# Attention values as unrounded matmuls in two column halves, one group for every four query blocks

## The chip, the cores and the metric

The kernel runs on one core of one Trainium2 chip. The metric is the device time of one execution in microseconds, the median of the runs of a kernel. Before the change that is 1438.92 us over 3 runs (1438.23 to 1439.44). Trace and page come from one further execution of the same kernel.

## The reference

One residual block on 1024 tokens of width 1024, in float32. Two branches share a normalised input; the change touches only the first of them, the stick-breaking attention with 8 heads of 64 columns:

```python
xn = rmsnorm(x, norm1_g)
q_sb, k_sb, v_sb, f_raw, i_hg, q_hg, g_hg, gate_sb, gate_hg = split(xn @ w_in)
# per head, per block of 128 queries
z = einsum('qd,kd->qk', q, k) * 64 ** -0.5
mask = kpos[None, :] < qpos[:, None]                     # strictly causal
log_beta = log_sigmoid(z)
log_rem = where(mask, log_beta - z, 0.0)
between = cumsum(log_rem, reverse=True) - log_rem
w = where(mask, exp(log_beta + between), 0.0)
o_sb = einsum('qk,kd->qd', w, v)                         # the part that changes
# the second branch: a gated linear recurrence over 4 heads of 128 (HGRN2), o_hg
merged = sigmoid(gate_sb) * (o_sb @ w_o_sb) + sigmoid(gate_hg) * (o_hg @ w_o_hg)
h = x + merged @ w_out
h = h + square(relu(rmsnorm(h, norm2_g) @ w_ff1)) @ w_ff2
out = rmsnorm(h, final_g)
```

## The kernel before

**Precision.** TensorE takes two kinds of operands here. Rounded ones (type fp32r) go through quickly but lose low bits, so a matrix is kept as a rounded part (suffix `h` or `H`, "hi") and a remainder (suffix `l` or `L`, "lo"). `hi_copy` makes the hi part with a copy on ScalarE (L144), `lo_sub` subtracts it from the source on VectorE (L149), and `hi_lo` does both. A product of two split matrices is three matmuls (hi·hi, hi·lo, lo·hi). Plain f32 operands are also taken, unrounded; the second branch uses them (tiles `sl`, `pkv`, `pho`).

**Stages.** First 58 us: the norm, the turned input `xn`, and the first projections. From 58 to 315 us: attention, 64 items (8 heads, query blocks in the order 7, 0, 6, 1, 5, 2, 4, 3), with the projections of the later heads and of the second branch filled in between ("fill"). Then the second branch, the merge, the output projection, and the two MLP products.

**One item** (head `h`, query block `qb` of 128 queries) goes through four functions. `scores` multiplies queries and keys into PSUM banks `z` and takes two sigmoids into `bt` and `rm` (ScalarE). `weights` forms the running product along the keys by a scan and multiplies it into `bt` (VectorE, L777 and L157). `turn` transposes `bt` in pieces of 128x128 on TensorE (bank `pw`, L124) and splits what comes out into `wTh` (ScalarE) and `wTl` (VectorE). `values` multiplies the turned weights with the head's values into bank `po`. The loop over items calls `weights` for the next item, `scores` for the one after it, some fill, and then `turn` of this item; `values` of a group that became complete runs in the item after that.

**Values before.** A group is a pair of query blocks, `qc` from 0 to 3, with `2*qc+2` key blocks. `v_epilogue` stores the values of a head as 64 hi columns beside 64 lo columns, so that a stationary operand of 128 columns holds both. For each key block there are two matmuls of 256 query columns, one against `wTh` and one against `wTl`: 320 matmuls in all (2+4+6+8 key blocks, times 2, times 8 heads). The upper and lower 64 rows of `po` are then added: ScalarE copies one half to `ot` (L850), VectorE adds the other (L851) into `osb`. Where the second block of a pair has one key block more than the first, `turn` has GpSimd clear the missing piece of `wTh` and `wTl` (L811).

**Order.** Each engine takes its instructions in program order. TensorE has two lanes, "main" (attention) and "fill"; a gate holds fill back until the main block two before it. `after(a, b)` only fixes an order on one engine: `turn_lo` holds the last remainder subtraction of a turn, and some scans and multiplies of `weights` are placed behind it. DMA loads are issued by SP in the order of the program; GpSimd issues the DMAs that copy QH and QL to the upper rows (L663) between its memsets.

**Memory.** Tiles of 128x1024 come from a pool of 40 slots, tiles up to 512 columns from 10 half slots; PSUM has 8 banks.

Of the kernel before, what the change touches and what calls it, by code (L numbers as in the profile page):

```python
# [9 lines left out]
F32 = mybir.dt.float32  # L10
# [9 lines left out]
P = 128  # L20
# [19 lines left out]
def kernel(  # L40
# [34 lines left out]
    def slot(name, dt=F32):  # L75
        return spool.tile([P, 1024], dt, tag="s", name=name)
# [75 lines left out]
    def hi_lo(h, l, src):  # L152
        hi_copy(h, src)
        return lo_sub(l, src, h)
# [493 lines left out]
    def v_stat(h, tb):  # L648
        c = ((tb % 2) * 4 + h % 4) * P
        return vt[h // 4, tb // 2][:, c : c + P]  # L650

    def qk_epilogue(h):
        def ep(ps, half):
# [80 lines left out]
    lastsel, turn_lo = [None], [None]  # L734

    def scores(h, qb):
        open_block("main")
# [29 lines left out]
    def weights(h, qb):  # L767

        nk = (qb + 1) * P
        bt, rm = zs[h, qb]
        cut = qb == NT - 1
        parts = ((512, nk - 1), (0, 512)) if cut else ((0, nk - 1),)
        for i, (a, b) in enumerate(parts):
            rr = rm[:, a:b][:, ::-1]
            sc = nc.vector.tensor_tensor_scan(  # L777
                out=rr,
                data0=rr,
                data1=bits[:, 1024 - nk + a : 1024 - nk + b][:, ::-1],  # L780
                initial=rm[:, b : b + 1] if i else 0.0,
                op0=ALU.mult,
                op1=ALU.max,
            )
            if i == 1 or (qb == 5 and h in (2,)):
                after(sc, turn_lo[0])
            m = mul(bt[:, a:b], bt[:, a:b], rm[:, a:b])
            if qb == 5:
                after(m, turn_lo[0])

    def turn(h, qb, between):

        open_block("main")
        bt, rm = zs.pop((h, qb))
        qc, par = qb // 2, qb % 2
        nkb = 2 * qc + 2
        if (h, qc) not in wTt:
            wTt[h, qc] = [
                tuple(
                    slot_n(f"wT{n}{h}_{qc}_{k0}", 256 * min(nkb - k0, 4), F32R).rearrange(  # L800
                        "p (k q) -> p k q", q=256
                    )
                    for n in "hl"
                )
                for k0 in range(0, nkb, 4)
            ]
        tiles = wTt[h, qc]
        qs = slice(par * P, (par + 1) * P)
        if par == 0:
            for t in tiles[-1]:  # L810
                after(nc.gpsimd.memset(t[:, (nkb - 1) % 4, qs].bitcast(F32), 0.0), lastsel[0])  # L811
        order = list(enumerate(tiles))
        for i, (th, tl) in order[::-1] if qb == NT - 1 else order:
# [13 lines left out]
            turn_hi[0] = hi_last[0]  # L827
        seen[h, qc] = seen.get((h, qc), 0) + 1
        return (h, qc) if seen[h, qc] == 2 else None

    def values(h, qc):
        open_block("main")
        tiles = wTt.pop((h, qc))
        nkb = 2 * qc + 2
        po = bank(f"po{h}_{qc}")[:, 0:256]
# [12 lines left out]
        other = DHS - r  # L848
        tmp = slot_n(f"ot{h}_{qc}", 256)[:, 0:256]
        nc.scalar.copy(tmp[r : r + DHS, :], po[other : other + DHS, :])  # L850
        nc.vector.tensor_tensor(  # L851
            out=osb[pair][r : r + DHS, qc * 256 : (qc + 1) * 256],
            in0=po[r : r + DHS, :],
            in1=tmp[r : r + DHS, :],
            op=ALU.add,
        )


    hg, ohg = {}, {}
# [101 lines left out]
    def hg_levels(h):  # L961

        dec, k, q = (hg[h, n] for n in ("pp", "k", "q"))
        sc = hg[h, "sc"] = slot(f"sc{h}")
        near = slot_n(f"near{h}", NT * Q)[:, 0 : NT * Q]
        nc.gpsimd.memset(near, 0.0)
        nc.gpsimd.memset(sc, 0.0)

        def scores_of(l, size, firsts, where):

            open_block("main")
            S = bank(f"sl{h}_{l}")
            for i, (s0, t0) in enumerate(firsts):
                r0, c0 = where(i, s0)
                matmul(
                    S[r0 : r0 + size, c0 : c0 + size],
                    k[:, s0 : s0 + size],
                    q[:, t0 : t0 + size],  # L980
                    start=True,
                    stop=True,
                )
            return S

        def near_scores(l):
# [12 lines left out]
        after(keep(5, S), turn_lo[0])  # L999
        yield  # L1000
        for l in range(7):
            H = 1 << l
            n = 512 // H
            if l < 5:
                S = near_scores(l)
            elif l == 5:
                S = scores_of(
                    l,
                    H,
                    [(s0, s0 + H) for s0 in range(0, T, 2 * H)],  # L1010
                    lambda i, s0: (s0 % P, s0 // P * H),
                )
# [12 lines left out]
            if l < 5:  # L1025
                keep(l, S)
            elif l == 5:
                for b in range(0, P, Q):
                    nc.scalar.copy(chunks(sc)[b : b + Q, :, b : b + Q], chunks(near, Q)[b : b + Q])
                for b in range(0, P, 2 * H):  # L1030
                    nc.scalar.copy(
                        chunks(sc)[b : b + H, :, b + H : b + 2 * H],
                        chunks(S[b : b + H, 0 : NT * H], H),
                    )
            else:
                for i in range(2):
# [1063 lines left out]
    for i, it in enumerate(items):  # L2100
# [150 lines left out]
```

## Time and profile before

| What | Value |
|---|---|
| median of 3 runs | 1438.92 us (1438.23 to 1439.44) |
| profiled execution | 1437.51 us, of which the span of instructions is 1435.7 us |
| granted TensorE clock | 0.998 |
| TensorE (PE) busy | 1421.1 us, 99% of the span |
| weight loads (PEld) | 1202.9 us, 84% |
| VectorE (DVE) | 1048.5 us, 73% |
| ScalarE (ACT) | 666.7 us, 46% |
| GpSimd (POOL) | 148.4 us, 10% |
| HBM | 162.55 MB read, 61.87 MB written |

Matmuls are pipelined: the time of one row runs from its start to the end of its last result, and the next one starts before that. What a matmul costs TensorE is therefore read from start to start of neighbouring rows, not from the duration of one. A plain f32 matmul stands in the trace as two records (two weight loads, two matmuls), a rounded one as one.

### The profile page before, as it was taken

Reading aid. Unit: us, or ns where it says so; the run is one execution under the profiler, and the core shown is the slowest. Engines: PE = TensorE matmul, PEld = TensorE weight load, DVE = VectorE, ACT = ScalarE, POOL = GpSimd, SP = SyncE. Lnnn points to the kernel's source line nnn. Section 1 sums busy time; section 2 is a strip of 40 time slices with the busy share of each in tenths; the row PEclk is TensorE's granted clock in tenths of the full one; section 3 lists DMA queues with packets and bytes.
Section 4 is the critical chain, followed back from the end, with each engine's and each line's share of the span. In section 5 each row is a group of like instructions: output and inputs, shape, how many; then the busy total and the mean of one; then the engine's idle time right before and its main releaser. Section 6 shows DMA issues by size and latency. Waiting matters only on the chain.

```text
span 1435.7 us, 22472 instructions
## 1 busy us (share of the span) xinstructions
PE 1421.1 (99%) x8774; PEld 1202.9 (84%) x8774; DVE 1048.5 (73%) x1432; ACT 666.7 (46%) x1164; POOL 148.4 (10%) x347
## 2 busy tenths in 40 slices
PE   9999999999999999999989999999999999999998
PEld 8989988987898888888878888888888888888886
DVE  6699899785635677877749897666666758668765
ACT  7566666542322344433335674544444433524343
POOL 3121121120001013000010300000000000000042
PEclk9999999999999999999999999999999999999999
DMA  7234154321303359754487405444446974776724
GB/s 213 49 93 110 37 95 83 60 45 53 104 16 104 91 173 259 233 170 154 154 246 275 176 30 198 140 140 142 159 154 223 344 261 161 271 274 248 271 103 180
DMA packets 157922, 225.89 MB, mean 157 GB/s; under 512 B 25676, under 2 KB 93816, under 8 KB 157816
## 3 DMA queue, kind: packets, MB, share of 16 engines
q1 hardware_dynamic: 142552, 183.29, 38.0%
q0 software_dynamic: 11520, 34.61, 9.7%
q10 hardware_dynamic: 3744, 6.56, 1.2%
q8 instruction: 69, 1.13, 0.3%
q14 instruction: 37, 0.30, 0.1%
HBM read 162.55 MB, written 61.87 MB: 156 GB/s over the span
## 4 chain that ended last, share of the span: by engine, by line
PE 95%; DMA 1%; issue 1%; POOL 1%; DVE 1%; ACT 1%; SPq 0%; POOLq 0%; DVEq 0%
PE pm L121 21%; PE pX L121 9%; PE pW L121 6%; PE pY L121 6%; PE pjqk L121 6%; PE pji L121 3%; PE pga L121 3%; PE pjq L121 3%; PE pjf L121 3%; PE pys L121 3%; PE gX L121 3%; PE pyh L121 3%; PE gY L121 3%; PE pjg L121 3%; PE po L121 3%; PE z L121 2%
## 5 line engine op out<-in xcount | busy, mean ns | idle before, releaser
L144 ACT CAST whid<-w 128x1024 fp32r<-128x1024 f32 x30 | 31.6, 1053 | 155.2 <-PE pm L121 91.0
L777 DVE TENSOR_TENSOR_SCAN rm<-rm,bits 128x511 f32<-128x511 f32 (+7 forms) x72 | 87.3, 1219 | 14.2 <-ACT rm L755 12.7
L121 PE MATMUL pm<-wlod,sh 128*128 128x512 f32 x240 | 93.5, 390 | 0.0
L121 PE MATMUL pm<-whid,sh 128*128 128x512 f32 x240 | 93.4, 389 | 0.0
L121 PE MATMUL pm<-whid,sl 128*128 128x512 f32 x240 | 93.4, 389 | 0.0
L121 PE MATMUL pm<-tl,sh 128*128 128x512 f32 (+1 forms) x210 | 81.3, 387 | 0.0
L121 PE MATMUL pm<-th,sl 128*128 128x512 f32 (+1 forms) x210 | 81.3, 387 | 0.0
L121 PE MATMUL pm<-th,sh 128*128 128x512 f32 (+1 forms) x210 | 81.3, 387 | 0.0
L149 DVE TENSOR_TENSOR wlod<-w,whid 128x1024 fp32r<-128x1024 f32 x30 | 36.7, 1223 | 57.6 <-ACT whid L144 57.3
L149 DVE TENSOR_TENSOR sl<-sa,sh 128x1024 fp32r<-128x1024 f32 x56 | 68.2, 1218 | 1.0 <-ACT sh L144 1.0
L144 ACT CAST wTh<-pw 128x128 fp32r<-128x128 f32 (+3 forms) x96 | 44.4, 487 | 52.7 <-PE pw L124 45.2
L1900 POOL TENSOR_SCALAR fss<-fss 128x1 f32<-128x1 f32 x8 | 4.5, 561 | 562.1 <-ACT fsc L1895 561.6
L144 ACT CAST sh<-sa 128x1024 fp32r<-128x1024 f32 x56 | 57.2, 1045 | 4.7 <-DMA sa<-ad 3.4
L149 DVE TENSOR_TENSOR wTl<-pw,wTh 128x512 fp32r<-128x512 f32 (+3 forms) x96 | 50.6, 547 | 9.7 <-ACT wTh L144 7.2
L121 PEld LDWEIGHTS pm<-wlod,sh 128*128 128x128 f32 x240 | 45.1, 188 | 10.0 <-DVE wlod L149 0.4
L121 PEld LDWEIGHTS pm<-whid,sl 128*128 128x128 f32 x240 | 45.1, 188 | 9.2
L121 PEld LDWEIGHTS pm<-whid,sh 128*128 128x128 f32 x240 | 45.0, 187 | 9.3
L157 DVE TENSOR_TENSOR bt<-bt,rm 128x511 f32<-128x511 f32 (+7 forms) x72 | 48.9, 685 | 5.1 <-ACT bt L758 1.0
L121 PE MATMUL pX<-sql,t1h 128*128 128x512 f32 x128 | 50.0, 391 | 0.1
L121 PE MATMUL pX<-sqh,t1h 128*128 128x512 f32 x128 | 49.8, 389 | 0.0
L121 PE MATMUL pX<-sqh,t1l 128*128 128x512 f32 x128 | 49.8, 389 | 0.0
L755 ACT ACTIVATE rm<-z 128x511 f32<-128x511 f32 (+6 forms) x96 | 47.5, 501 | 4.5 <-DVE bt L157 1.9
(912 smaller groups left out, 4486.9 us busy)
## 6 DMA issues: line engine op xcount, KB each, us to landing
w<-in_w_ff_dram SPq DMA_DIRECT2D x72, 512.0 KB, 4.9
sa<-ad SPq DMA_DIRECT2D x56, 512.0 KB, 6.6
ad<-a SPq DMA_DIRECT2D x32, 256.0 KB, 4.4
ad<-s SPq DMA_DIRECT2D x16, 512.0 KB, 5.7
tw<-in_w_out_dram POOLq DMA_DIRECT2D x24, 256.0 KB, 4.1
x<-in_x_dram SPq DMA_DIRECT2D x8, 512.0 KB, 8.5
xnl<-xnh POOLq DMA_DIRECT2D x8, 512.0 KB, 9.9
pr<-pd SPq DMA_DIRECT2D x8, 512.0 KB, 6.0
```

The costliest lines, as they stand in the source:

```text
L121: return pe(nc.tensor.matmul(*a, **k))
L144: hi_last[0] = after(in_turn("act", nc.scalar.copy(dst, src)), hi_behind[0])
L149: nc.vector.tensor_tensor(out=dst, in0=src, in1=hi.bitcast(F32), op=ALU.subtract),
L157: return nc.vector.tensor_tensor(out=out, in0=a, in1=b, op=ALU.mult)
L755: nc.scalar.activation(rm[:, s0 + c0 - 1 : s0 + m - 1], z[:, c0:m], AF.Sigmoid, scale=-0.125)
L777: sc = nc.vector.tensor_tensor_scan(out=rr, data0=rr, data1=bits[:, 1024 - nk + a : 1024 - nk + b][:, ::-1], initial=rm[:, b : b + 1] if i ...
L1900: nc.gpsimd.tensor_scalar(out=ssq, in0=ssq, scalar1=1.0 / D, scalar2=EPS, op0=ALU.mult, op1=ALU.add)
```

## The change

Values and turned weights are no longer split. `v_epilogue` copies the values as f32 (64 columns a head), `turn` copies the transposed weights as f32 into a single tile `wT`; the subtractions on VectorE and the GpSimd memsets are gone. `values` works on four query blocks at once: a big pair (`qc` 3 or 2) and the small one (`3 - qc`, that is 0 or 1). Each matmul has a stationary operand of 64 columns; even key blocks write the lower 64 rows of `po`, odd ones the upper 64, and the matmuls of one and the other half stand alternately. Pieces that the mask makes zero are left out: the last key blocks are multiplied with 128 of the 256 query columns, and one piece of them (`left`, the big pair's last even block) goes to the lower half. There are 11 matmuls a call, 7 of 256 query columns and 4 of 128, together 2304 columns; there are 16 calls in all (two a head). `turn_lo` is gone as an order constraint; what stood behind it now is free or stands behind the last multiply of `weights`.

```diff
         def ep(ps, tb):
-            if tb % 2 == 0:
-                vt[quad, tb // 2] = slot(f"V{quad}_{tb // 2}", F32R)
-            V = vt[quad, tb // 2].rearrange("p (t h s d) -> p t h s d", t=2, h=4, s=2)
-            src = ps.rearrange("p (h d) -> p h d", h=4)
-            hi_lo(V[:, tb % 2, :, 0, :], V[:, tb % 2, :, 1, :], src)
+            if tb % 4 == 0:
+                vt[quad, tb // 4] = slot(f"V{quad}_{tb // 4}")
+            hi_copy(vt[quad, tb // 4][:, tb % 4 * 256 : (tb % 4 + 1) * 256], ps)
...
-        if par == 0:
-            for t in tiles[-1]:
-                after(nc.gpsimd.memset(t[:, (nkb - 1) % 4, qs].bitcast(F32), 0.0), lastsel[0])
...
-            turn_lo[0] = hi_lo(
-                th[:, 0:n, qs], tl[:, 0:n, qs], pw[:, : n * P].rearrange("p (k q) -> p k q", q=P)
-            )
+            hi_copy(t[:, 0:n, qs], pw[:, : n * P].rearrange("p (k q) -> p k q", q=P))
             turn_hi[0] = hi_last[0]
-        seen[h, qc] = seen.get((h, qc), 0) + 1
-        return (h, qc) if seen[h, qc] == 2 else None
+        both = max(qc, 3 - qc)
+        seen[h, both] = seen.get((h, both), 0) + 1
+        return (h, both) if seen[h, both] == 4 else None
...
-    def values(h, qc):
+    def values(h, big):
         open_block("main")
...
-        for kb in range(nkb):
-            for i in range(2):
-                matmul(
-                    po,
-                    v_stat(h, kb),
-                    tiles[kb // 4][i][:, kb % 4, :],
-                    start=kb == 0 and i == 0,
-                    stop=kb == nkb - 1 and i == 1,
-                )
+        last = 2 * big
+        whole, left, right = slice(0, 256), slice(0, P), slice(P, 256)
+        order = []
+        for kb in range(0, last, 2):
+            order += [(big, kb, whole), (big, kb + 1, whole)]
+        for kb in range(0, 2 * small_, 2):
+            order += [(small_, kb, whole), (small_, kb + 1, whole)]
+        order += [(small_, 2 * small_, whole), (big, last, right), (big, last + 1, right)]
+        order += [(big, last, left), (small_, 2 * small_ + 1, right)]
...
+        where = [(qc, (kb % 2) if cs is not right else 1) for qc, kb, cs in order]
...
+            r = key[1] * DHS
+            matmul(
+                po[qc][r : r + DHS, cs],
+                v_stat(h, kb),
+                tiles[qc][kb // 4][:, kb % 4, cs],
+                start=key not in begun,
+                stop=left_over[key] == i,
+            )
...
+        for qc in (big, small_):
+            cs = right if qc == 0 else whole
...
+            nc.scalar.copy(tmp[r : r + DHS, cs], src[other : other + DHS, cs])
+            if qc == 0:
+                nc.scalar.copy(dst[r : r + DHS, left], src[0:DHS, left])
+            nc.vector.tensor_tensor(
+                out=dst[r : r + DHS, cs],
...
-        after(keep(5, S), turn_lo[0])
+        keep(5, S)
...
-            attended[0] = turn_lo[0]
+            attended[0] = weighted[0]
```

Two places of the order on the engines, both around the first head's query blocks 1 to 5. In the names `po_3` is the bank of pair 3, `wT_3_0` the turned weights of pair 3 from key block 0 on, `V_0` the values; the last number of a name only counts tiles.

On TensorE, before: `values` of pair 3 stands behind the transposes of block 1 (a hi and a lo matmul for each of eight key blocks, of which the first two and the last are shown), and `values` of pair 0 behind those of block 5.

```order
L124 MATMUL pw_1_0_945<-ident,bt_1_833 128x128 x2
L121 MATMUL po_3_950<-wTh_3_0_813,V_0_329 128x256
L121 MATMUL po_3_950<-wTl_3_0_814,V_0_329 128x256
...
L121 MATMUL po_3_950<-wTl_3_4_816,V_3_711 128x256
L121 MATMUL z_4_0_975<-KS_453,QH_451 128x320
...
L124 MATMUL pw_5_1_1009<-ident,bt_5_874 128x128 x2
L121 MATMUL po_0_1014<-wTh_0_0_864,V_0_329 128x256
L121 MATMUL po_0_1014<-wTl_0_0_865,V_0_329 128x256
...
L121 MATMUL z_3_0_1026<-KS_453,QH_451 128x512
```

And of the change:

```order
L124 MATMUL pw_1_0_923<-ident,bt_1_819 128x128 x2
L121 MATMUL z_4_0_931<-KS_451,QH_449 128x320
...
L124 MATMUL pw_5_1_962<-ident,bt_5_856 128x128 x2
L121 MATMUL po_3_966<-wT_3_0_803,V_0_329 64x256 x4
L121 MATMUL po_3_966<-wT_3_4_804,V_1_651 64x256 x2
L121 MATMUL po_0_967<-wT_0_0_850,V_0_329 64x256
L121 MATMUL po_3_966<-wT_3_4_804,V_1_651 64x128 x3
L121 MATMUL po_0_967<-wT_0_0_850,V_0_329 64x128
L121 MATMUL z_3_0_991<-KS_451,QH_449 128x512
```

The sixteen matmuls of pair 3 moved from behind block 1 to behind block 5 and stand in one run with those of pair 0; everything else on TensorE keeps its place.

On VectorE, before, from block 1's multiply to the sum of pair 0:

```order
L157 TENSOR_TENSOR bt_1_833<-bt_1_833,rm_1_834 128x255
L149 TENSOR_TENSOR wTl_0_0_865<-pw_0_0_868,wTh_0_0_864 128x128
L777 SCALAR_TENSOR_TENSOR rm_5_875<-rm_5_875,bits 128x767
L149 TENSOR_TENSOR wTl_3_0_814<-pw_6_0_901,wTh_3_0_813 128x4x128
L149 TENSOR_TENSOR wTl_3_4_816<-pw_6_1_908,wTh_3_4_815 128x3x128
L157 TENSOR_TENSOR bt_5_874<-bt_5_874,rm_5_875 128x767
...
L149 TENSOR_TENSOR wTl_0_0_865<-pw_1_0_945,wTh_0_0_864 128x2x128
L851 TENSOR_TENSOR osb_967<-po_3_950,ot_3_968 64x256
L157 TENSOR_TENSOR bt_2_916<-bt_2_916,rm_2_917 128x383
...
L851 TENSOR_TENSOR osb_967<-po_0_1014,ot_0_1019 64x256
```

And of the change:

```order
L157 TENSOR_TENSOR bt_1_819<-bt_1_819,rm_1_820 128x255
...
L775 SCALAR_TENSOR_TENSOR rm_5_857<-rm_5_857,bits 128x767
L157 TENSOR_TENSOR bt_5_856<-bt_5_856,rm_5_857 128x767
L775 SCALAR_TENSOR_TENSOR rm_2_895<-rm_2_895,bits 128x383
L157 TENSOR_TENSOR bt_2_894<-bt_2_894,rm_2_895 128x383
...
L157 TENSOR_TENSOR bt_4_929<-bt_4_929,rm_4_930 128x639
L859 TENSOR_TENSOR osb_979<-po_3_966,ot_3_980 64x256
L859 TENSOR_TENSOR osb_979<-po_0_967,ot_0_983 64x128
```

The remainders between a scan and its multiply are gone, and the sums of both pairs stand together behind block 4's multiply.

More of the change, by code (lines that the diff above doesn't have):

```diff
@@ L639, in ep @@
         def ep(ps, tb):
-            if tb % 2 == 0:
-                vt[quad, tb // 2] = slot(f"V{quad}_{tb // 2}", F32R)
-            V = vt[quad, tb // 2].rearrange("p (t h s d) -> p t h s d", t=2, h=4, s=2)
-            src = ps.rearrange("p (h d) -> p h d", h=4)
-            hi_lo(V[:, tb % 2, :, 0, :], V[:, tb % 2, :, 1, :], src)
+            if tb % 4 == 0:
+                vt[quad, tb // 4] = slot(f"V{quad}_{tb // 4}")
+            hi_copy(vt[quad, tb // 4][:, tb % 4 * 256 : (tb % 4 + 1) * 256], ps)
         return ep
     def v_stat(h, tb):
-        c = ((tb % 2) * 4 + h % 4) * P
-        return vt[h // 4, tb // 2][:, c : c + P]
+        c = ((tb % 4) * 4 + h % 4) * DHS
+        return vt[h // 4, tb // 4][:, c : c + DHS]
     def qk_epilogue(h):
@@ L733 @@
     zs, wTt, seen = {}, {}, {}
-    lastsel, turn_lo = [None], [None]
+    lastsel, weighted = [None], [None]
     def scores(h, qb):
@@ L776, in weights @@
             rr = rm[:, a:b][:, ::-1]
-            sc = nc.vector.tensor_tensor_scan(
+            nc.vector.tensor_tensor_scan(
                 out=rr,
@@ L784, in weights @@
             )
[L785 to L789, printed above, removed]
+            weighted[0] = mul(bt[:, a:b], bt[:, a:b], rm[:, a:b])
     def turn(h, qb, between):
@@ L798, in turn @@
             wTt[h, qc] = [
-                tuple(
-                    slot_n(f"wT{n}{h}_{qc}_{k0}", 256 * min(nkb - k0, 4), F32R).rearrange(
-                        "p (k q) -> p k q", q=256
-                    )
-                    for n in "hl"
+                slot_n(f"wT{h}_{qc}_{k0}", 256 * min(nkb - k0, 4)).rearrange(
+                    "p (k q) -> p k q", q=256
                 )
@@ L808, in turn @@
         qs = slice(par * P, (par + 1) * P)
-        if par == 0:
-            for t in tiles[-1]:
-                after(nc.gpsimd.memset(t[:, (nkb - 1) % 4, qs].bitcast(F32), 0.0), lastsel[0])
         order = list(enumerate(tiles))
-        for i, (th, tl) in order[::-1] if qb == NT - 1 else order:
+        for i, t in order[::-1] if qb == NT - 1 else order:
             n = min(qb + 1 - 4 * i, 4)
@@ new lines, in turn @@
+            turn_hi[0] = hi_last[0]
+        both = max(qc, 3 - qc)
+        seen[h, both] = seen.get((h, both), 0) + 1
+        return (h, both) if seen[h, both] == 4 else None
+    def values(h, big):
+        open_block("main")
+        small_ = 3 - big
+        tiles = {qc: wTt.pop((h, qc)) for qc in (big, small_)}
+        po = {qc: bank(f"po{h}_{qc}")[:, 0:256] for qc in (big, small_)}
+        last = 2 * big
[7 more added lines that the diff above has]
+        order += [(big, last, left), (small_, 2 * small_ + 1, right)]
+        begun, left_over = set(), {}
+        where = [(qc, (kb % 2) if cs is not right else 1) for qc, kb, cs in order]
+        for i, key in enumerate(where):
+            left_over[key] = i
+        for i, ((qc, kb, cs), key) in enumerate(zip(order, where)):
+            r = key[1] * DHS
[5 more added lines that the diff above has]
+                stop=left_over[key] == i,
+            )
+            begun.add(key)
@@ L848, in values @@
         other = DHS - r
[L849 to L856, printed above, removed]
+        for qc in (big, small_):
+            cs = right if qc == 0 else whole
+            src, dst = po[qc], osb[pair][:, qc * 256 : (qc + 1) * 256]
+            tmp = slot_n(f"ot{h}_{qc}", 256)[:, 0:256]
+            nc.scalar.copy(tmp[r : r + DHS, cs], src[other : other + DHS, cs])
[3 more added lines that the diff above has]
+                out=dst[r : r + DHS, cs],
+                in0=src[r : r + DHS, cs],
+                in1=tmp[r : r + DHS, cs],
+                op=ALU.add,
+            )
     hg, ohg = {}, {}
```

5 lines of the change are left out of this document (removed).

## The prediction

> **What bounds the kernel now.** I read the page first, then the stretches by stage, then what TensorE waited for, and last the order of time on TensorE at the lines that change.
>
> ```profile
> span 1435.7 us, 22472 instructions
> PE 1421.1 (99%) x8774; PEld 1202.9 (84%) x8774; DVE 1048.5 (73%) x1432; ACT 666.7 (46%) x1164; POOL 148.4 (10%) x347
> PE 95%; DMA 1%; issue 1%; POOL 1%; DVE 1%; ACT 1%; SPq 0%; POOLq 0%; DVEq 0%
> core 0: us, PE busy (x) PEld busy (x) DVE busy (x) ACT busy (x) POOL busy (x), PEclk, DMA share, GB/s
> 0.00:58.00 58.00, 55.25 (x393) 51.81 (x394) 36.30 (x70) 35.53 (x71) 13.70 (x35) 1.00 0.53 151
> 58.00:315.00 257.00, 256.88 (x1659) 231.30 (x1661) 226.75 (x326) 166.11 (x384) 52.10 (x187) 1.00 0.35 74
> ```
>
> TensorE holds 95% of the chain that ended last. In attention, 58 to 315 us, it is idle for 0.12 us of 257. VectorE is busy for 226.75 us there: much, but nothing waits for it, as the waits of the weight loads up to 320 us show.
>
> ```profile
> PEld pjqk L121 <- DVE xnl L325: 0.7, 2, 0.5
> PEld po L121 <- POOL wTh L811: 0.5, 2, 0.3
> PEld z L121 <- DVE wTl L149: 0.2, 1, 0.2
> ```
>
> The columns are total, times, longest. So the change is worth what it saves or adds in TensorE's own work, plus these few tenths.
>
> **The old values, removed.** The counts come from the groups, the price from start to start in the order of time (first column).
>
> ```profile
> L121 PE MATMUL po<-wTh,V 128*128 128x256 f32 x160 | 42.4, 299 | 0.1
> L121 PE MATMUL po<-wTl,V 128*128 128x256 f32 x160 | 39.7, 283 | 0.0
> 68.67 0.28 PE L121 MATMUL po<-wTl,V 128*128 128x256 f32 x1
> ...
> 70.33 0.28 PE L121 MATMUL po<-wTl,V 128*128 128x256 f32 x1
> 70.45 0.31 PE L121 MATMUL z<-KS,QH 128*128 128x320 f32 x1
> ```
>
> From the second of sixteen (68.67) to the scores behind them (70.45) fifteen starts pass in 1.78 us, 0.119 us each. 320 of them are 38.0 us. That term goes.
>
> **The new values, added.** The trace of before has unrounded matmuls in the second branch, of full width and in column parts. Full width first: seven matmuls of 128 columns, two records each.
>
> ```profile
> 371.90 0.39 PE L121 MATMUL pjf<-xnl,wf2h 128*128 128x512 f32 x1
> 372.13 0.39 PE L121 MATMUL pjf<-xnh,wf2l 128*128 128x512 f32 x1
> 372.36 1.72 PE L121 MATMUL pkv<-v,pp 128*128 128x128 f32 x14
> 373.84 0.48 PE L121 MATMUL pjf<-xnh,wf2h 128*128 128x512 f32 x1
> 374.15 0.40 PE L121 MATMUL pjf<-xnl,wf2h 128*128 128x512 f32 x1
> ```
>
> A rounded matmul of 512 columns takes 0.23 us (371.90 to 372.13). From 372.36 to 374.15 are 1.79 us; less the one rounded matmul in it, seven unrounded ones cost 1.56 us: 0.223 us for 128 columns, 1.74 ns a column. A new call has 2304 columns, 4.01 us if each matmul has the array to itself, and 2.00 us if the two halves run side by side throughout. Both halves carry 1152 columns, so the split itself is even.
>
> Whether they run side by side, and what surrounds such a run, is shown by the second branch's scores in two column halves: eight matmuls of 64 columns, alternating halves as the change does.
>
> ```profile
> 352.36 0.39 PE L121 MATMUL pga<-xnh,wga0wlo 128*128 128x512 f32 x1
> 352.68 0.69 PE L121 MATMUL sl<-q,k 128*64 128x64 f32 x16
> 353.29 0.50 PE L121 MATMUL pga<-xnh,wga0whi 128*128 128x512 f32 x1
> 353.62 0.39 PE L121 MATMUL pga<-xnl,wga0whi 128*128 128x512 f32 x1
> 353.14 0.22 PE L121 MATMUL sl<-q,k 128*64 128x64 f32 x1
> ```
>
> (The last row is from a narrower window and shows the last record of the sixteen.) One after another, 512 columns would take 0.89 us. From 352.68 to 353.14 fifteen of sixteen records pass in 0.46 us: the halves do run side by side, at half the price of 0.445 us plus a tenth. But the run costs more than that: 352.36 to 353.62 is 1.26 us, less two rounded matmuls (0.46) leaves 0.80 us. So 0.36 us is a fixed price of going into such a run and out of it: the first record starts 0.09 late, the rounded matmul behind it needs 0.33 instead of 0.23, and the rest is the pipeline that empties and fills. The four-way run agrees.
>
> ```profile
> 319.56 0.39 PE L121 MATMUL pjf<-xnh,wf1l 128*128 128x512 f32 x1
> 319.88 0.76 PE L121 MATMUL sl<-q,k 128*32 128x32 f32 x64
> 320.57 0.51 PE L121 MATMUL pjf<-xnh,wf1h 128*128 128x512 f32 x1
> 320.91 0.39 PE L121 MATMUL pjf<-xnl,wf1h 128*128 128x512 f32 x1
> ```
>
> 1024 columns are 1.78 us in a row; 319.56 to 320.91 less 0.46 is 0.89 us, a quarter (0.445) and 0.445 us around it.
>
> One call of the change is then 2.00 + 0.36 = 2.36 us, sixteen calls 37.8 us: **0.2 us less** than the 38.0 that go. No row shows a run of 256 columns, so I bound it. Above: if in such a run each matmul's second record can start only behind its first, and the other half's only behind that, the first record and the last pieces of a run stand alone; that costs one record of 256 columns, 256 x 1.74 / 2 = 0.22 us, a call 2.58 us, all of them 41.3: 3.3 us more. Below: if going in and out were free between transposes (which are unrounded too), 2.00 x 16 = 32.0: 6.0 us less. I take the middle value, by the row with two halves, which is the nearest; its tenth, if it grew with the length, would be 0.2 us a call and lies within the upper bound.
>
> **The waits that go.** GpSimd's memsets of `wTh` and `wTl` are gone, and so is VectorE's link between transpose and values. Two places show what they cost.
>
> ```profile
> 248.19 0.28 PE L121 MATMUL po<-wTl,V 128*128 128x256 f32 x1
> 248.47 0.39 PE L121 MATMUL po<-wTh,V 128*128 128x256 f32 x1
> 281.51 0.28 PE L121 MATMUL po<-wTl,V 128*128 128x256 f32 x1
> 281.91 0.39 PE L121 MATMUL po<-wTh,V 128*128 128x256 f32 x1
> ```
>
> 0.28 and 0.40 us from start to start instead of 0.12: 0.44 us. I count -0.45; the end on the other side is 0, if the grouped call waits for something else instead.
>
> **VectorE and ScalarE.** The remainders leave VectorE:
>
> ```profile
> L149 DVE TENSOR_TENSOR wTl<-pw,wTh 128x512 fp32r<-128x512 f32 (+3 forms) x96 | 50.6, 547 | 9.7 <-ACT wTh L144 7.2
> L149 DVE TENSOR_TENSOR V<-pjv,V x16: 401/416/425, 18.3 to 161.3; 128x256 fp32r<-128x256 f32 x16
> L850 ACT COPY ot<-po x32: 364/368/372, 70.7 to 315.0; 64x256 f32<-64x256 f32 x32
> L851 DVE TENSOR_TENSOR osb<-po,ot x32: 392/422/428, 73.1 to 315.4; 64x256 f32<-64x256 f32 x32
> ```
>
> 50.6 + 16 x 0.416 = 57 us of work, a quarter of what VectorE does in attention. On the path it is worth almost nothing, since TensorE's work covers it: the 0.2 us that `z` waited for a remainder, and at most the 0.7 us that the first projections waited for `xnl`, in front of which the first remainders of the values stand. I count -0.2 (0 to -0.9). ScalarE makes as many copies of turned weights as before, and eight more of at most 0.37 us for pair 0: 3 us on an engine that is busy 166 of 257, hidden by TensorE. If that cover were gone it would be these 3 us. The banks `po` wait longer for their sums, since two come at once; behind them stand `z` and `pw` that need a bank, but VectorE has a quarter less in front of those sums. Nothing.
>
> The sum is -0.2 - 0.45 - 0.2 = -0.85 us. The profiled execution of 1437.51 us (span 1435.7 and 1.8 around it) becomes 1436.7, and as the median of the runs stood 1.4 above that execution, **1438.0 us** is my forecast for it. The likeliest case alone runs from 1438.92 - 0.2 - 0.45 - 0.9 = 1437.4 to 1438.92 + 3.3 = 1442.2.
>
> **Rivals.**
>
> *Long column halves overlap less than short ones* (slower). Two streams of 256 columns read from SBUF at once, while those of the trace are 64 and 32 columns long. For it: the four-way run needs 0.69 us from its first start to the next rounded one; less the 0.15 us by which that one trails the last record in the two-way run (353.14 to 353.29), some 0.54 us for 1.78 us of work, 3.3 streams of 4, or 0.8. Against it: the two-way run loses only a tenth. At 0.8 a call is 4.01 / 1.6 + 0.36 = 2.87 us, all of them 45.9: +7.9 - 0.65 gives **1446.2**. Without any overlap a call is 4.37 us, 69.9 in all, about 1470. It decides as slower once the sum exceeds +2.9 us, that is below 1.79 streams of 2. The Trainium skill, "TensorE: Matmul & The Clock Gate", section "Measured speedup vs the span model", lists 2.38 times for three column tiles, 0.79 of three; taken for two, an estimate from that page is 4.01 / 1.59 + 0.36 = 2.88 us a call, +8 us. The two-way row speaks against it, at nine tenths.
>
> *The run's entry and exit are hidden* (faster). For it: before and behind the new runs stand transposes and scores, not a dense stream of rounded matmuls. Against it: the 0.36 us stands in the trace of before around each run of that kind that I looked at. 32.0 instead of 38.0, less 0.65: **1432.3**. From 2.22 us a call down it counts as faster.
>
> *The grouped call comes too early* (slower by a little): the last block turned of a group is needed one item later, as before, but then twice the matmuls stand behind its copy. If each of 16 calls waited 0.3 us, the longest wait in the row of L811, +4.8 us would come: 1443. A whole item of about 4 us (257 / 64) lies between, so I think little of it.
>
> **How the numbers follow.** No change, as forecast: 0.56. Less overlap: 0.18. Entry and exit hidden, or more won from VectorE than the waits show: 0.20. The early group: 0.06. With 0.2% (2.9 us) as what a measurement can tell from no change, faster is 0.21 (the second rival and a little of the first case), same 0.55, slower 0.24 (the two slower rivals). The range takes in the second rival's side down to 1432.5 and the first up to 1446; outside lie the hidden entry in full and a lost overlap.
>
> **What would show it.** `po` from start to start: 11 matmuls (22 records) in about 2.1 us, two records at a time, and a call's share between transposes and scores of 2.3 to 2.6 us. PE still idle for less than 0.5 us from 58 to 315, DVE there near 170 us, no row with L811, and the second branch beginning within 1 us of 315. A call near 2.9 us or above makes the first rival right, 2.0 the second; PE waits on `wT` or on a bank make the third. What would prove the whole argument wrong is a gain that lies outside the values, at the rounded projections or in a later stage.

## The result, and the profile after

The changed kernel takes 1436.03 us (median of 13 runs, 1434.32 to 1438.42), the kernel before 1438.49 us (13 runs, 1436.59 to 1439.61). The ratio is 0.9983 [0.9975, 0.9992]: 2.5 us less, inside the 0.2% that counted as no change, but with an interval that leaves out 1. The profiled execution took 1435.34 us, 2.17 less than the one of before.

The page of the changed kernel (span, busy time), and its stretches up to the end of attention (window, its length, busy time and instructions of PE, PEld, DVE, ACT, POOL, then clock, DMA share, GB/s):

```profile
span 1433.3 us, 22366 instructions
PE 1418.9 (99%) x8806; PEld 1188.9 (83%) x8806; DVE 999.7 (70%) x1320; ACT 666.8 (47%) x1172; POOL 138.5 (10%) x283
```

```profile
0.00:58.00 58.00, 55.50 (x393) 52.27 (x394) 35.17 (x63) 35.63 (x71) 13.36 (x33) 1.00 0.53 151
58.00:315.00 257.00, 257.00 (x1750) 219.16 (x1750) 180.88 (x223) 165.31 (x392) 43.01 (x125) 1.00 0.36 76
```

TensorE is still the bound: its 0.12 us of idle time in attention have become zero. VectorE lost 46 us there (226.75 to 180.88), and the whole got 2.5 us shorter.

The new values stand on TensorE like this. First a call of pairs 3 and 0 between transposes and scores, then one of pairs 2 and 1 between two sets of transposes, in order of time (start, duration, and the count of records at the end):

```profile
71.75 0.82 PE L124 MATMUL pw<-ident,bt 128*128 128x128 f32 x6
72.49 2.17 PE L121 MATMUL po<-wT,V 128*64 128x256 f32 x22
74.59 0.50 PE L121 MATMUL z<-KS,QH 128*128 128x512 f32 x1
74.93 0.40 PE L121 MATMUL z<-KS,QL 128*128 128x512 f32 x1
...
88.66 2.17 PE L121 MATMUL po<-wT,V 128*64 128x256 f32 x22
90.76 0.66 PE L124 MATMUL pw<-ident,bt 128*128 128x128 f32 x4
```

A call needs 2.10 us from its first start to the next matmul behind it (72.49 to 74.59, 88.66 to 90.76). All sixteen calls do so to within 0.01 us. The records start in pairs from the first one on. Two narrower windows of the first call give the pace:

```profile
72.49 0.44 PE L121 MATMUL po<-wT,V 128*64 128x256 f32 x2
...
72.49 1.73 PE L121 MATMUL po<-wT,V 128*64 128x256 f32 x14
```

The first pair ends at 72.93, the seventh at 74.22: six pairs in 1.29 us, 0.215 us for two records of 256 columns, one of each half. In the run with one half first, below, a record that runs alone takes as long. So an unrounded matmul, two records, that has the array to itself costs 1.68 ns a column.

Where the second branch begins says what attention as a whole has won. The rows give the instructions of its first scores (`sl_d`, durations, first and last start), first of the kernel before, then of the changed one:

```profile
L121 PE MATMUL sl_d<-q,k x64: 196/196/218, 314.9 to 315.4; 128*32 128x32 f32 x64
```

```profile
L121 PE MATMUL sl_d<-q,k x64: 196/196/217, 312.1 to 312.7; 128*32 128x32 f32 x64
```

314.87 against 312.13 in the trace: 2.74 us earlier. Not all of that belongs to attention. The last projection in front of the first values, which both kernels have, starts at these times before and after:

```profile
65.59 0.40 PE L121 MATMUL pjqk<-xnh,wqk1l 128*128 128x512 f32 x1
65.45 0.40 PE L121 MATMUL pjqk<-xnh,wqk1l 128*128 128x512 f32 x1
```

So 0.14 us are there before any value is multiplied, and 2.60 us arise behind it. Over all the runs of this document this start lies between 65.35 and 65.93 us, so where a difference at the second branch is small I also give it from this row on. Up to 608 us the lead is 3.0 us (one wait of the second branch, 0.24 us before `sl` at 341.40, is gone too), and at the end 2.4. So the change is won in attention, and about half a microsecond of it is given back in the last stages. Those run the same instructions, and 0.5 us is an eighth of the spread of single runs, so I draw nothing from it.

What TensorE's weight loads waited for up to 320 us in the changed kernel (total, times, longest):

```profile
PEld po L121 <- issue: 2.3, 14, 0.2
...
PEld z L121 <- issue: 1.4, 8, 0.2
PEld pw L124 <- issue: 1.0, 6, 0.2
...
PEld pjqk L121 <- DVE xnl L325: 0.5, 1, 0.5
```

The rows with L811 and with `wTl` are gone. In their place stand 28 short waits for nothing that the profile shows, of at most 0.2 us: 14 at `po` and 14 at the `z` and `pw` behind. By their counts they are entries into the sixteen runs and exits from them.

### The profile page after: what moved, and what is told of

The parts are those of the page before. It is cut to its first block, busy times and chain, and to the rows that moved or that the text cites. A ratio compares the mean times of both kernels' runs of the same rounds, so it can differ in the third digit from the quotient of the medians.

```text
span 1433.3 us, 22366 instructions
## 1 busy us (share of the span) xinstructions
PE 1418.9 (99%) x8806; PEld 1188.9 (83%) x8806; DVE 999.7 (70%) x1320; ACT 666.8 (47%) x1172; POOL 138.5 (10%) x283
## 4 chain that ended last, share of the span: by engine, by line
PE 45%; DVE 1%; POOL 1%; DMA 1%; issue 1%; ACT 1%; POOLq 0%; DVEq 0%
PE pm L121 19%; PE pX L121 9%; PE pY L121 6%; PE pW L121 6%; PE pwX L121 2%; PE pwY L121 2%; PE pwW L121 1%; DMA h<-in_x_dram 1%; PE hnt L124 0%; POOL fss L1912 0%; PE pyh L121 0%; ACT fsc L1903 0%; DVE wlod L149 0%; DVE w L1155 0%; PE gX L121 0%
## 5 line engine op out<-in xcount | busy, mean ns | idle before, releaser
L144 ACT COPY wT<-pw 128x128 f32<-128x128 f32 (+3 forms) x96 | 43.8, 483 | 47.6 <-PE pw L124 45.5
L753 ACT ACTIVATE rm<-z 128x511 f32<-128x511 f32 (+4 forms) x96 | 47.8, 500 | 1.9 <-PE z L121 1.6
L756 ACT ACTIVATE bt<-z 128x512 f32<-128x512 f32 (+3 forms) x96 | 47.9, 500 | 0.3 <-PE pw L124 0.3
```

The costliest lines, as they stand in the source:

```text
L144: hi_last[0] = after(in_turn("act", nc.scalar.copy(dst, src)), hi_behind[0])
L753: nc.scalar.activation(rm[:, s0 + c0 - 1 : s0 + m - 1], z[:, c0:m], AF.Sigmoid, scale=-0.125)
L756: nc.scalar.activation(bt[:, s0 : s0 + e], z[:, :e], AF.Sigmoid, scale=0.125)
```

## The experiments

After the result my theory was this. The values cost 16 calls of some 2.28 us, 36.4 us instead of the 38.0 that went. The remaining microsecond is waits behind GpSimd's memsets and VectorE's remainders. VectorE's relief as such is worth nothing. The rivals: that VectorE's relief is the gain after all, that alternation of the halves doesn't matter, that going in and out costs nothing, and that its price depends on the neighbours.

### VectorE's work put back

The remainders of turned weights and of values are subtracted again, into a slot that nothing reads. The values on TensorE stay as in the change.

```diff
-            hi_copy(vt[quad, tb // 4][:, tb % 4 * 256 : (tb % 4 + 1) * 256], ps)
+            V = vt[quad, tb // 4][:, tb % 4 * 256 : (tb % 4 + 1) * 256]
+            hi_copy(V, ps)
+            lo_sub(slot(f"Vl{quad}_{tb}", F32R)[:, 0:256], ps, V)
...
-            hi_copy(t[:, 0:n, qs], pw[:, : n * P].rearrange("p (k q) -> p k q", q=P))
+            src = pw[:, : n * P].rearrange("p (k q) -> p k q", q=P)
+            hi_copy(t[:, 0:n, qs], src)
+            unread = slot(f"wTl{h}_{qb}_{i}", F32R)
+            lo_sub(unread[:, : n * P].rearrange("p (k q) -> p k q", q=P), src, t[:, 0:n, qs])
```

> The change with VectorE's removed work put back: every remainder of values and of turned weights is subtracted again, into a tile that nobody reads; the matmuls are those of the change. Theory (the gain is TensorE's own work, about 1.6 us cheaper values and 0.7 us of waits at rounded values): the run stays within 1 us of the change, ratio to before 0.998 to 0.999, and the second branch still begins near 312 us. Rival (the gain is VectorE's relief of 57 us): it goes back to before, ratio 1.000, second branch near 315 us.

Measured: 1436.53 us (11 runs) beside 1438.57 us of before, ratio 0.9983 [0.9974, 0.9992], the same as the change itself. Its stretch of attention, the longest wait that the changed kernel does not have, and its `sl_d`:

```profile
58.00:315.00 257.00, 256.82 (x1748) 218.77 (x1747) 226.00 (x326) 165.09 (x392) 42.59 (x125) 1.00 0.36 76
```

```profile
PEld z L121 <- DVE QL L149: 0.8, 2, 0.6
```

```profile
L121 PE MATMUL sl_d<-q,k x64: 195/196/218, 312.8 to 313.3; 128*32 128x32 f32 x64
```

VectorE is again busy for 226.0 us in attention, as before (226.75), and nearly all of the gain stays. The second branch starts 0.64 us later than in the changed kernel. Of these, 0.18 are there at the last projection in front of the values (65.64 instead of 65.45). The other 0.46 arise almost wholly at one place: a `z` at 126.08 us waits for QL, in front of which the remainders stand; it starts 0.34 us late and the matmul behind it another 0.10. The other new waits are of 0.2 us at most and leave no step in the starts on TensorE. VectorE's relief as such is worth at most this half microsecond. The run doesn't test the links, since no matmul reads these remainders.

### The old values without the remainder of the turned weights

The kernel before, with the old 320 matmuls, but without VectorE's remainders of the turned weights. The second matmul of each key block takes the rounded part again, so the weights count twice and lack their remainder; the remainders of the values stay. With the tiles `wTl` their clearing goes too, so that GpSimd has 31 instructions less in attention (156 instead of 187).

```diff
-                    for n in "hl"
+                    for n in "h"
...
-            turn_lo[0] = hi_lo(
-                th[:, 0:n, qs], tl[:, 0:n, qs], pw[:, : n * P].rearrange("p (k q) -> p k q", q=P)
-            )
+            hi_copy(th[:, 0:n, qs], pw[:, : n * P].rearrange("p (k q) -> p k q", q=P))
...
-                    tiles[kb // 4][i][:, kb % 4, :],
+                    tiles[kb // 4][0][:, kb % 4, :],
```

> The kernel before with VectorE's remainders of the turned weights left out: the second matmul of each key block uses the rounded part again, so the values lack the remainder of the weights. TensorE has the same 320 matmuls, VectorE 50 us less. Theory: only the waits at the values go, 0.5 to 1 us, ratio to before 0.9993 to 0.9997. Rival (VectorE's relief is the gain): 2.4 us, ratio 0.998.

Measured: 1437.89 us (11 runs) beside 1438.04 (14 runs), ratio 0.9994 [0.9985, 1.0003]. Attention and the start of the second branch:

```profile
58.00:315.00 257.00, 257.00 (x1710) 231.91 (x1710) 185.30 (x233) 166.60 (x384) 48.17 (x156) 1.00 0.36 76
```

```profile
L121 PE MATMUL sl_d<-q,k x64: 196/196/218, 313.8 to 314.4; 128*32 128x32 f32 x64
```

VectorE falls to 185 us, and the second branch starts 1.05 us earlier (314.87 to 313.82 in the trace). In the whole time no difference can be told from none. Again 0.14 us of the 1.05 are there by the last projection in front of the values (65.45), so 0.91 belong to attention. Most of them are the two places that the prediction names. Here is the rest of the first, in the kernel before, from the stalled matmul on:

```profile
248.47 0.39 PE L121 MATMUL po<-wTh,V 128*128 128x256 f32 x1
248.69 0.30 PE L121 MATMUL po<-wTl,V 128*128 128x256 f32 x1
248.83 0.39 PE L121 MATMUL z<-KS,QH 128*128 128x512 f32 x1
```

The start behind the stall comes 0.22 us later, not 0.12, and the one behind that 0.14. So the first place costs 0.28 us and the second, at 281.91, 0.41; in this run TensorE gains just these amounts there. The remaining 0.2 us come in steps of about 0.1 or less. Whether VectorE's remainders or GpSimd's memsets held up these two places the run doesn't separate, since both are fewer in it; the row of before that names such waits names the memsets (L811).

This splits the change: 0.14 us lie before attention, 0.91 are waits that go with the second tile of weights, and the 1.69 from here to the changed kernel (313.82 to 312.13; both start attention at 65.45) are the values themselves. 38.0 - 1.69 is 36.3 us, 2.27 us a call.

### All matmuls of one half first

The changed kernel, with the matmuls of a call sorted: first all that write the lower rows, then all for the upper ones.

```diff
+        order.sort(key=lambda o: 1 if o[2] is right else o[1] % 2)
```

> The change with the matmuls of a call sorted: first all that write the lower half, then all of the upper half. Theory (halves run side by side only where they alternate): a call streams 2304 columns at 1.74 ns, 4.0 us instead of 2.0, 32 us more in sixteen calls, ratio to before about 1.020. Rival (the array keeps a queue for each half, so that order does not matter): the time of the change, 0.998.

Measured: 1456.61 us (2 runs), ratio 1.0125 [1.0107, 1.0144]. The first call, whole, and then in three narrower windows (its first record alone, up to 73.73, and up to 73.745 us); last, a call of pairs 2 and 1 up to 91.22 and up to 91.235:

```profile
72.39 3.52 PE L121 MATMUL po<-wT,V 128*64 128x256 f32 x22
75.83 0.50 PE L121 MATMUL z<-KS,QH 128*128 128x512 f32 x1
...
72.39 0.43 PE L121 MATMUL po<-wT,V 128*64 128x256 f32 x1
72.39 1.51 PE L121 MATMUL po<-wT,V 128*64 128x256 f32 x6
72.39 1.78 PE L121 MATMUL po<-wT,V 128*64 128x256 f32 x8
...
89.88 1.51 PE L121 MATMUL po<-wT,V 128*64 128x256 f32 x6
89.88 1.78 PE L121 MATMUL po<-wT,V 128*64 128x256 f32 x8
```

```profile
L121 PE MATMUL sl_d<-q,k x64: 195/196/218, 333.3 to 333.9; 128*32 128x32 f32 x64
```

A call needs 3.44 us to the next matmul instead of 2.10. Sixteen times 1.34 is 21.4, and the second branch starts 21.2 us later. So it is the order that makes the two halves run side by side throughout. But the loss is only two thirds of the 2.0 us a call that a run without any overlap would lose, and the windows show why: six records pass alone, up to 73.73 (0.216 us each: 1.51 less 0.43, in five steps), and 0.015 us later two more have started. The lower half has ten records in this call, so these are its seventh and the first of the upper half, which stands four places behind it. The upper half begins as soon as the running record is four places ahead of its own first one, and the last records of the lower half overlap with it. All sixteen calls do the same at the seventh record. A change of bank is not the cause: in calls of pairs 3 and 0 the lower half goes over to the other bank at its seventh record, but in those of pairs 2 and 1 already at its fifth. It also means that TensorE starts matmuls of the two halves out of program order: the upper half's first record starts before three of the lower half that stand in front of it. That an engine takes its instructions in program order holds here only for each half by itself.

### Two and two

That reading asks for a test: the same matmuls with two of the lower rows behind each other and then two of the upper rows, so that four records of one half follow one another (near the end of a call, where two of the upper rows already stood together, six).

```diff
+        for j in range(0, len(order) - 3, 4):
+            order[j + 1], order[j + 2] = order[j + 2], order[j + 1]
```

> The changed kernel, but within a call two matmuls of the lower rows stand behind each other and then two of the upper rows, instead of one and one. In the run with all matmuls of one half first, the other half began when four records of the first were left. Theory (the array takes records of the other half only from the next three or four behind the running one): four records of one half in a row are just within that reach, a call's 22 records start within 1.9 to 2.15 us (1.90 in the changed kernel), the second branch starts at most 4 us later than 312.1 us, and the time is at most 1440 us. Rival (only the very next record can start beside the running one, and what lies behind it waits): of four records three would run alone, a call's records would take about 0.75 of the serial 4.0 us, 2.9 us or more, and the second branch would start some 16 us later, the time near 1452 us.

Measured: 1438.34 us beside 1438.02 of before (one run each, so no interval). The first call, and `sl_d`:

```profile
72.61 2.22 PE L121 MATMUL po<-wT,V 128*64 128x256 f32 x22
74.76 0.50 PE L121 MATMUL z<-KS,QH 128*128 128x512 f32 x1
```

```profile
L121 PE MATMUL sl_d<-q,k x64: 196/196/217, 312.9 to 313.4; 128*32 128x32 f32 x64
```

2.15 us instead of 2.10 in all sixteen calls, and 0.75 us later at the second branch (16 x 0.05 = 0.8; 0.63 from the last projection in front of the values on). The theory holds: four places ahead are within reach. The rival's 2.9 us is refuted. Why the reach ends there no run shows.

### Groups of two query blocks

Each pair of query blocks gets a call of its own again, as in the kernel before: 32 calls instead of 16, with the same matmuls. Within a call the halves are no longer even, since only one of the two gets the last piece of 256 columns and the other one of 128.

```diff
-        both = max(qc, 3 - qc)
-        seen[h, both] = seen.get((h, both), 0) + 1
-        return (h, both) if seen[h, both] == 4 else None
+        seen[h, qc] = seen.get((h, qc), 0) + 1
+        return (h, qc) if seen[h, qc] == 2 else None
...
+        order += [(big, last, whole), (big, last + 1, right)]
```

> The unrounded halves with groups of two query blocks as before: 32 calls instead of 16. The longer half of a call has 256*(qc+1) columns, 2560 a head instead of 2304, 0.45 us a head more; and each call pays the way in and out, 0.28 us, twice as often, 0.56 us a head more. Theory: 8 us more than the change, ratio to before about 1.004. Rival (the way in and out costs nothing beside transposes): 3.6 us more, ratio 1.001.

Measured: 1443.72 us (6 runs), ratio 1.0033 [1.0021, 1.0045]. Calls of pairs 3, 0 and 2, the last run of the last head, and `sl_d`:

```profile
68.44 1.94 PE L121 MATMUL po<-wT,V 128*64 128x256 f32 x16
70.31 0.41 PE L121 MATMUL z<-KS,QH 128*128 128x320 f32 x1
...
74.50 0.65 PE L121 MATMUL po<-wT,V 128*64 128x256 f32 x4
75.08 0.50 PE L121 MATMUL z<-KS,QH 128*128 128x512 f32 x1
...
85.08 1.51 PE L121 MATMUL po<-wT,V 128*64 128x256 f32 x12
86.52 0.50 PE L121 MATMUL z<-KS,QH 128*128 128x512 f32 x1
...
317.88 2.37 PE L121 MATMUL po<-wT,V 128*64 128x256 f32 x20
```

```profile
L121 PE MATMUL sl_d<-q,k x64: 196/196/218, 320.2 to 320.7; 128*32 128x32 f32 x64
```

Pairs 3 and 0 together need 1.87 + 0.58 = 2.45 us to the next matmul, where the changed kernel needs 2.10. The second branch starts 8.05 us later than in the changed kernel. Of these, 16 x 2 uneven halves at 0.11 us each (128 columns of 1.68 ns, half of which would vanish in an even split) are 3.5, and 4.5 us remain for the additional entries and exits. In the last head the calls of pairs 2 and 1 follow each other without anything between (20 records in one run), so there are 31 runs instead of 16: 0.30 us for each of the fifteen. Entry and exit are not free.

### All four pairs of a head at once

The other direction: one call for the eight query blocks of a head, 8 calls instead of 16, with four banks for `po`.

```diff
-        both = max(qc, 3 - qc)
-        seen[h, both] = seen.get((h, both), 0) + 1
-        return (h, both) if seen[h, both] == 4 else None
+        seen[h] = seen.get(h, 0) + 1
+        return (h, 0) if seen[h] == 8 else None
...
+        po = {qc: bank(f"po{h}_{qc}")[:, 0:256] for qc in (3, 0, 2, 1)}
...
+        for big, small_ in ((3, 0), (2, 1)):
```

> The values of a whole head in one call: 8 calls instead of 16, the same columns. Theory (each way in and out costs 0.28 us): 2.2 us less than the change, ratio to before 0.9968. Rival (a run of 4.2 us and four banks at once hold up scores and transposes): no gain, or slower than the change, with waits of z or pw on banks.

Measured: 1432.56 us (5 runs), ratio 0.9960 [0.9947, 0.9972] to the kernel before. The interval lies wholly below that of the change (0.9975 to 0.9992), so this version beats both kernels. A call, and `sl_d`:

```profile
86.80 4.12 PE L121 MATMUL po<-wT,V 128*64 128x256 f32 x44
90.85 0.66 PE L124 MATMUL pw<-ident,bt 128*128 128x128 f32 x4
```

```profile
L121 PE MATMUL sl_d<-q,k x64: 196/196/217, 309.6 to 310.2; 128*32 128x32 f32 x64
```

44 records need 4.05 us to the next matmul, where two calls of 22 need 4.20, and each of the two also a late start in front and a slow matmul behind. The second branch starts 2.54 us earlier than in the changed kernel, although this trace is 0.48 us behind it at the last projection in front of the values (65.93 instead of 65.45). From there on the gain is 3.02 us, 0.38 us for each of the eight entries and exits saved. One short row names a bank (`pw` behind the sum into `osb`, once, 0.2 us), no longer than the other seven exits; the rival's long waits did not come, though four banks are held at once. The median fell by 3.5 us.

### The call between dense rounded matmuls

Before these last runs I put the low price of entry and exit down to the neighbours: transposes are unrounded, and beside them the change of kind might cost less. Here `values` stands one place earlier, directly behind the scores and in front of the fill.

```diff
+        before = ready.popleft() if ready else None
+        if before:
+            values(*before)
         if i % 2 == 1:
             next(wsums, None)
...
         def between():
-            if before:
-                values(*before)
+            pass
```

> The changed kernel, but the values of a group stand one place earlier on TensorE, directly behind the scores and in front of the rounded projections, so that dense rounded matmuls and not transposes surround them. Read at the eight calls of pairs 3 and 0, whose matmuls keep their order. Theory (going into and out of an unrounded run costs the 0.36 us of the earlier traces beside dense rounded matmuls, and only 0.25 to 0.31 beside transposes, which are unrounded themselves): from the last rounded start before such a call to the first one behind it, less that matmul's own price, 2.33 to 2.40 us. Rival (the price is lower because the run is longer, whatever stands around it): 2.25 to 2.30 us, as in the changed kernel. The whole time says little, since waits can come or go with the place: 1434 to 1440 us by both.

Measured: 1436.18 us in a single run. The first call in order of time:

```profile
68.75 0.31 PE L121 MATMUL z<-KS,QH 128*128 128x320 f32 x1
68.90 0.30 PE L121 MATMUL z<-KS,QL 128*128 128x320 f32 x1
69.14 2.17 PE L121 MATMUL po<-wT,V 128*64 128x256 f32 x22
71.24 0.50 PE L121 MATMUL pjqk<-xnh,wqk2h 128*128 128x512 f32 x1
71.57 0.39 PE L121 MATMUL pjqk<-xnl,wqk2h 128*128 128x512 f32 x1
```

From 68.90 to 71.57 are 2.67 us. Less the scores' own 0.15 (68.75 to 68.90) and 0.23 for the rounded projection, 2.29 us remain, which is what the rival named. Of these, 0.09 us lie before the first record (0.24 less 0.15) and 0.10 in the slow rounded matmul behind (0.33 less 0.23), just as around the short run in the trace of before. So the neighbours in front make no difference; my theory of the transposes falls. It is right for the matmul behind alone: the second transpose behind a call starts 0.165 us after the first, some 0.06 late, the rounded one 0.10. All eight calls of pairs 3 and 0 in this run agree: seven come to 2.29 or 2.30 us, and the one that has transposes behind it to 2.25. The rival has the number, but its reason needs a closer look: the way in and out costs what it cost in the trace of before, and what is cheaper is the stream, as the next section works out.

## Why the prediction was right, and where not

The forecast was 1438.0 us and no change; 1436.03 came, 2.0 us less. Of these, 0.4 lie in the kernel before, whose median fell from 1438.92 to 1438.49 with more runs; the change itself was foretold at -0.85 us and came to -2.46. That is 0.4 us inside the bound of 2.9, so the verdict owes something to the width of the bound. (A call would have counted as faster from 2.23 us down, by the prediction's own terms, not 2.22.) Point by point:

- **TensorE bounds, VectorE is worth nothing.** Right. VectorE lost 46 us in attention, and with that work put back 0.46 us of the 2.60 of attention were lost again, nearly all through one wait. (The 170 us foretold for VectorE became 181. Durations of its instructions in the window fell by 56 us in sum, 242 to 186, but neighbouring ones overlap, and busy time counts an overlap once.)
- **The old values, 38.0 us.** Right: the run with the old values and the changed kernel differ by 1.69 us at the second branch; 38.0 less eight calls of 2.30 us and eight of 2.25, read from start to start, is 1.6.
- **Two halves side by side throughout.** Right: records start in pairs, and 2304 columns pass at half their price. The rival of less overlap in long halves falls, and so does the upper bound, a first record that stands alone. The Trainium skill's 2.38 of three streams ("TensorE: Matmul & The Clock Gate", "Measured speedup vs the span model"), behind that rival, doesn't carry over to two: here it was two of two. What makes it so is the order: with one half first, a call takes 1.34 us more.
- **"So 0.36 us is a fixed price of going into such a run and out of it", a call 2.36 us.** The mechanism is right, and the price about right: nearly twice as many runs cost 0.30 us for each one more, half as many save 0.38 for each one less, and the rival "hidden" falls. But a call came to 2.30 us before scores, 2.25 before transposes, 2.27 by the second branch. The term that was mis-sized is mainly the stream, 2.00 us. It took 1.74 ns a column from seven matmuls of 128 columns; at the 1.68 of the long run it is 1.94 us. What is left of a call is then 0.36 us before scores, just as foretold, and 0.31 before transposes, where the slow matmul behind the run costs 0.04 us less. Over both kinds of call that is 0.08 of the 0.09 us by which a call is cheaper. Sixteen of them are 1.4 us: -1.7 for the values instead of -0.2. The length of the pieces explains only a part of the 1.74: the records of 128 columns in the new calls follow one another at 0.109 us, 1.70 ns a column, those of `pkv` at 0.111. Why those cost more no run shows.
- **The waits that go, -0.45, and VectorE's links, -0.2.** Right in kind, too small: the run without the second tile of weights gained 0.91 us in attention. The two places alone gave 0.28 + 0.41 = 0.69 us. I had counted only the stall itself (0.16 + 0.28) and not the two matmuls behind it, which start 0.10 and 0.02 us late. Another 0.2 came in steps too short to stand among the rows, and 0.24 us went within the second branch.
- **The early group.** The grouped call waited for nothing: no row with `wT` or a bank stands in the changed kernel's waits up to 320 us.

By measured terms the sum is -1.69 for the values, -0.91 for waits in attention, -0.14 before it and -0.24 within the second branch, or -3.0 us, which is the lead at 608 us; -2.4 of it are left at the end of the profiled execution, and -2.46 in the medians. The outcome is "no change" by the bound that I had set, and a small, real gain by the interval.

## What to carry to other kernels

Where unrounded matmuls replace split ones at nearly equal column time, as here, what decides is how often TensorE goes from one kind of matmul to the other: gather them into fewer, longer runs (here 32, 16 and 8 calls gave 1443.7, 1436.0 and 1432.6 us). Let column halves alternate closely. Price a run as a part per column and a part per run, and expect the first, taken from another kind of matmul, to be off by some per cent (1.74 against 1.68 ns). Count with a stall the slow starts behind it. And when you compare two traces at a late row, compare them at an early one too: start-up alone put the runs here up to 0.6 us apart.

## What the runs showed of the hardware that I had not expected

- A record of the other column half starts beside the running one when it stands up to four places behind it in TensorE's order: in alternation by two records and by four the halves overlap (2.10 and 2.15 us to the next matmul), and with one half's ten records first, the other began with the seventh in all sixteen calls (3.44 us), ahead of three records that stand before it in the program.
- Two column halves of 256 columns lose nothing to each other: 0.215 us for a pair of records, one of each half, and 0.216 for a single one where one half runs alone.
